# The output projection of a hybrid encoder layer: three blocks of 512 tokens and columns of 512 against two halves of 768 tokens and columns of 1024

## The chip, the core and the metric

The kernel runs on one core of a Trainium2 chip. The metric is the device time of one execution in microseconds (us), the median of several runs; less is better. TensorE (PE) multiplies matrices, VectorE (DVE), ScalarE (ACT) and GpSimd (POOL) work on tiles in the on-chip memory, and SyncE (SP) here only issues DMA transfers. The five engines each run their own list of instructions in order and wait for one another by semaphores.

## The reference, cut to what matters

The layer normalises the tokens (1,024 of a prompt and 512 of a sample, 1,536 in all, width 2,048), projects them with `w_in`, runs three kinds of attention, multiplies each branch by a gate and joins them to `y` (1,536 x 2,048). What the change touches is the last line:

```
y = jnp.concatenate([ya, yb, yc], axis=-1) @ w_out     # w_out is 2048 x 2048, float32
return x + rmsnorm(y, post_gain)                       # mean of squares over the 2048 columns of a row
```

The product needs float32 accuracy, so each operand is split into a rounded part H and a remainder L, and a product is the sum of three: H by H, H by L, L by H.

## The kernel before

A first stage multiplies by `w_in` in three passes of 512 tokens (b = 0, 1, 2), then come attention stages, and `y` is left transposed in DRAM (`yT`). The last stage, lines 1546 to 1858, is the output projection, and `low`, `tail` and the pools named in its head are its on-chip memory.

**Tiling.** It goes over three blocks b of 512 tokens, and in each over four column blocks cb of 512. In a block both operands are cut in halves, and seven products (Strassen-Winograd, j = 0 to 6) take the place of eight. On the side of y the operands are A11, A12, S3, S1, S2, A22 and S4 (`OPS`), on the side of the weights two quarters as they are, one more, and four sums of quarters. The contraction of 1,024 is walked in quarters s = 0 to 3, so `columns(b, cb)` has 28 steps (s, j). A step first splits its weights, 128 x 512 numbers (`prep`, line 1680 on ACT makes wH, line 1681 on DVE wL), LEAD = 4 steps ahead, and then runs `product` (line 1689): 2 rows groups q x 2 slices c x 3 matmuls of 256 columns, 12 in all, with y as the stationary operand. The whole stage has 336 steps.

**Sums.** GpSimd makes the weight sums of every (b, cb, s) from freshly loaded weights (lines 1664, 1667, 1670, 1674) and the y sums of every block (line 1585). The y operands of a block stay on chip in split form (lines 1589 and 1590).

**Leaving.** `leave(j)` adds finished products into the result tile z (lines 1715 to 1729), `rows_squares` sums squares (line 1609), `gained` multiplies by the gain, and the rows go to DRAM (line 1739). When a block is through, `finish_load` (lines 1627, 1628), `finish_rows` (line 1634) and `finish_store` (line 1638) read z and x back, scale by one over the root, add x and store the output, spread over the following block. The last column block of the last block runs its seven products one after the other instead (`final`), with a tail written out by hand (`tail_*`).

**Order.** Two timelines, `before` and `after`, map a step to the small jobs that are issued ahead of it or behind it. The loop at the end walks the steps and issues all of it in this order on all engines (`IN_ORDER`); so each engine's list is what the code writes. SP has the loads and stores of the stage, and each of its DMAs also waits for the one eight places earlier in its queue, so at most eight are under way.

## Time and profile before

| what | value |
|---|---|
| runs | 3181.72, 3188.18, 3186.55 us; median 3186.55 us |
| the profiled execution | 3185.0 us, of which its span 3183.2 us |
| busy over the span | PE 2999.4 us (94%), DVE 2390.1 us (75%), ACT 1528.5 us (48%), POOL 962.9 us (30%) |
| the output projection | from 2567.15 us to the end of the span |
| DMA over the span | 649.93 MB, 204 GB/s |

The span is from the first to the last instruction on the chip in one profiled execution. A share of busy time is a mean over stages of different kinds: what bounds the last stage is read in its own stretch of the trace, and the chain of waits names what PE waited for. Moments below are microseconds from the start of the span.

### The profile page before, as it was taken

The page shows a single profiled execution, that of the slowest core. Times are in us where ns is not written, and L with a number is a line of the kernel's source. Part 1 is how long each engine was busy: PE and PEld are TensorE (multiplying, and loading weights), DVE is VectorE, ACT ScalarE, POOL GpSimd, SP SyncE. Part 2 cuts the span into 40 slices and gives each one's busy share as a digit, 9 for nine tenths or more (in the row PEclk, how much of TensorE's full clock was granted, in tenths as well). Part 3 has the DMA queues.
Part 4 walks back from the last instruction along what each step waited for, and adds up shares of the span by engine and source line. Part 5 has one row for each costly group of instructions (what it writes and reads, how often), then busy time and mean ns, then how long its engine had stood idle before and what let it go on. Part 6 is the DMA issues. An engine that isn't in the chain of part 4 may idle for free.

```text
span 3183.2 us, 57740 instructions
## 1 busy us (share of the span) xinstructions
PE 2999.4 (94%) x22030; PEld 2823.9 (89%) x22030; DVE 2390.1 (75%) x3887; ACT 1528.5 (48%) x3028; POOL 962.9 (30%) x607
## 2 busy tenths in 40 slices
...
GB/s 215 145 259 249 270 255 287 315 321 187 239 219 223 263 373 205 211 209 225 212 212 221 141 184 161 132 163 115 110 132 106 163 136 136 126 182 247 141 246 227
DMA packets 412335, 649.93 MB, mean 204 GB/s; under 512 B 38445, under 2 KB 247001, under 8 KB 388761
## 3 DMA queue, kind: packets, MB, share of 16 engines
...
## 4 chain that ended last, share of the span: by engine, by line
PE 63%; DVE 15%; DMA 7%; issue 6%; POOL 6%; ACT 2%; SPq 1%; DVEq 0%; POOLq 0%; ACTq 0%
PE m L453 34%; PE s L1332 5%; PE acc L822 4%; DMA w<-in_w_in_dram 4%; DVE wL L1681 4%; PE acc L1689 4%; PE o L1374 3%; PE acc L904 2%; PE m L269 2%; PE acc L1178 2%; PE pp L1352 2%; DVE wL L177 2%; PE acc L1025 2%; POOL w L429 1%; DVE S L1590 1%
## 5 line engine op out<-in xcount | busy, mean ns | idle before, releaser
L177 DVE TENSOR_TENSOR wL<-w,wH 128x512 fp32r<-128x512 f32 x576 | 451.6, 801 | 193.7 <-ACT wH L176 189.9
L176 ACT CAST wH<-w 128x512 fp32r<-128x512 f32 x576 | 349.2, 618 | 340.3 <-PE m L453 272.1
L1689 PE MATMUL acc<-wH,S 128*128 128x256 f32 x1536 | 306.2, 293 | 0.0
L180 DVE SCALAR_TENSOR_TENSOR wL<-w,wH 128x512 fp32r<-128x512 f32 x288 | 224.6, 790 | 107.8 <-ACT wH L179 104.6
L1681 DVE TENSOR_TENSOR wL<-w,wH 128x512 fp32r<-128x512 f32 x288 | 274.0, 976 | 36.1 <-ACT wH L1680 32.2
L1689 PE MATMUL acc<-wL,S 128*128 128x256 f32 x768 | 231.0, 301 | 70.4 <-DVE wL L1681 70.2
L179 ACT ACTIVATE wH<-w 128x512 fp32r<-128x512 f32 x288 | 178.7, 630 | 204.2 <-PE m L453 153.5
L1680 ACT CAST wH<-w 128x512 fp32r<-128x512 f32 x288 | 174.6, 618 | 205.0 <-PE acc L1689 78.2
L1689 PEld LDWEIGHTS acc<-wH,S 128*128 128x128 f32 x1536 | 259.6, 203 | 0.0
L1689 PEld LDWEIGHTS acc<-wL,S 128*128 128x128 f32 x768 | 155.9, 203 | 80.6 <-DVE wL L1681 80.5
L1689 PE MATMUL acc<-wH,A 128*128 128x256 f32 x1152 | 219.9, 281 | 0.2 <-ACT wH L1680 0.2
L992 POOL DMA_DIRECT2D dk<-kaT x8 | 4.5, 557 | 671.1 <-DMA craw<-cqT 485.2
L1689 PEld LDWEIGHTS acc<-wH,A 128*128 128x128 f32 x1152 | 184.5, 191 | 0.8 <-ACT wH L1680 0.8
L1689 PE MATMUL acc<-wL,A 128*128 128x256 f32 x576 | 164.5, 286 | 18.9 <-DVE wL L1681 18.8
L453 PE MATMUL m<-A12H,wL 128*128 128x256 f32 x576 | 166.7, 289 | 10.8 <-DVE wL L177 10.8
L453 PE MATMUL m<-S3H,wL 128*128 128x256 f32 x576 | 165.7, 288 | 7.8 <-DVE wL L177 6.1
L453 PE MATMUL m<-A22H,wL 128*128 128x256 f32 x576 | 165.4, 287 | 6.5 <-DVE wL L177 6.5
L453 PE MATMUL m<-S2H,wL 128*128 128x256 f32 x576 | 165.1, 287 | 4.1 <-DVE wL L177 4.1
L453 PE MATMUL m<-A12H,wH 128*128 128x256 f32 x576 | 167.5, 291 | 0.0
L453 PE MATMUL m<-A22H,wH 128*128 128x256 f32 x576 | 165.9, 288 | 0.0
L453 PE MATMUL m<-A12L,wH 128*128 128x256 f32 x576 | 165.8, 288 | 0.0
L453 PE MATMUL m<-S1H,wL 128*128 128x256 f32 x576 | 163.3, 284 | 2.2 <-DVE wL L177 2.2
...
## 6 DMA issues: line engine op xcount, KB each, us to landing
w<-w SPq DMA_DIRECT2D x144, 1024.0 KB, 8.1
w<-in_w_in_dram SPq DMA_DIRECT2D x96, 1024.0 KB, 8.6
w<-in_w_out_dram SPq DMA_DIRECT2D x94, 512.0 KB, 6.9
T<-w SPq DMA_DIRECT2D x96, 256.0 KB, 5.4
z<-z SPq DMA_DIRECT2D x38, 512.0 KB, 5.2
h<-hA SPq DMA_DIRECT2D x14, 1024.0 KB, 12.0
w<-T SPq DMA_DIRECT2D x48, 256.0 KB, 2.5
y<-yT SPq DMA_DIRECT2D x22, 512.0 KB, 7.0
```

The source lines that it names most:

```text
L176: nc.scalar.copy(H, src)
L177: engine.tensor_sub(L, src, f(H))
L179: nc.scalar.activation(H, src, AF.Copy, scale=scale)
L180: nc.vector.scalar_tensor_tensor(L, src, scale, f(H), op0=ALU.mult, op1=ALU.subtract)
L269: nc.tensor.matmul(a, lhsT=lhsT, rhs=rhs, start=(c == 0 and i == 0), stop=(c == NC_D - 1 and i == 2))
L453: nc.tensor.matmul(M[j], lhsT=w[:, c, :], rhs=h[:, 4 * i + c, :], start=(i == c == x == 0), stop=(i == 1 and c == 3 and x == 2))
L822: nc.tensor.matmul(a, lhsT=wt[:, c, :], rhs=ht[:, c, :], start=(c == 0 and i == 0), stop=(c == 3 and i == 2))
L1332: nc.tensor.matmul(S[:, c], lhsT=a[:, qs], rhs=b[:, c], start=(i == 0), stop=(i == len(pairs) - 1))
L1374: nc.tensor.matmul(o, lhsT=a[:, vs], rhs=b, start=(kc == 0 and i == 0), stop=(kc == n - 1 and i == 2))
L1680: nc.scalar.copy(H, src)
L1681: nc.vector.tensor_sub(L, src, f(H))
L1689: nc.tensor.matmul(m, lhsT=a[:, c, P * q:P * q + P], rhs=w[:, c, :], start=(first and c == x == 0), stop=(s == 3 and c == 1 and x == 2), s ...
```

## The change

The stage is written anew; the way of splitting, the seven products and the three-matmul product stay.

- **Tokens and columns.** Two halves of 768 tokens are A1 and A2 (t = 0, 1), and two column blocks cb = 0, 1 of 1,024 columns, each again in two halves of 512 (lo, hi). So all 1,536 tokens go through one set of seven products for each cb. A step is (j, cb, c) with c = 0 to 7 a slice of 128 of the contraction, and there are 112 steps. A step has 6 row groups q x 3 matmuls of 512 columns, 18 in all, and one split of 128 x 512 weights, LEAD = 2 steps ahead. The products come in three groups: j = 0 and 1 for both cb, then 4, 3 and 6, then 2 and 5.
- **Resident sums of y.** Three slots hold y operands in split form, each replaced piece by piece once its last step is through: slot 0 A11, then S1, then A22; slot 1 A12, then S4, then the last eight weights; slot 2 S2, then S3. The sums are made on GpSimd, 768 wide, in buffers of a ring of four (`y_raw`): S3, S1 and S2 of one c in steps 18, 20, ..., 32, where S2 also goes to DRAM through GpSimd's own DMA queue (`s2_store`); S4 in steps 36 to 46 with S2 read back; S3 again in steps 60 to 74.
- **Weight sums.** They are made once, on GpSimd, in the third pass of the `w_in` stage, every 18 steps of that pass for one of 16 pieces (`out_load`, `out_sums`, `out_store`), and lie in DRAM (`WO`).
- **Partial results.** j = 0, 4 and 3 leave partial results a, U and W (6 row groups x 512 columns for each cb) in DRAM; `load_part` brings them back for the products that add to them. `keep` sums squares, multiplies by the gain and stores a finished piece of z.
- **Finishing.** The first half's rows are finished in steps 81 to 94, from operand buffers that are free by then; the second half's rows after the last products, which run row group by row group (steps 104 to 111 for q = 0, then for q = 1, ...), each followed by its own `leave`, `inverse` and `finish`.

Taken from the diff, cut to its core:

```diff
+    WO = [[scratch(f"wo{n}{cb}", (P, 8 * 512)) for n in range(4)] for cb in range(2)]
...
+        def out_load(cb, c):
+            WOT[cb, c] = t = ring("wo", 2, 1024)
+            for k in range(2):
+                r = 1024 * k + P * c
+                nc.sync.dma_start(t[:, k, :], w_out[r:r + P, 1024 * cb:1024 * cb + 1024])
+            if c % 4 == 0:
+                WOT[cb, "t3"] = ring("wo3", 4, 512)
+        def out_sums(cb, c, i):
+            lo, hi = slice(0, 512), slice(512, 1024)
+            t, t3 = WOT[cb, c], WOT[cb, "t3"][:, c % 4, :]
+            sub = nc.gpsimd.tensor_sub
+            if i == 0:
+                sub(t3, t[:, 1, hi], t[:, 0, hi])
+            elif i == 1:
+                sub(t[:, 0, lo], t[:, 0, hi], t[:, 0, lo])
+            elif i == 2:
+                sub(t[:, 0, hi], t[:, 1, hi], t[:, 0, lo])
+            else:
+                sub(t[:, 1, lo], t[:, 1, lo], t[:, 0, hi])
+        def out_store(cb, c):
+            t = WOT.pop((cb, c))
+            for n, src in ((0, t[:, 0, :512]), (1, t[:, 0, 512:]), (3, t[:, 1, :512])):
+                nc.sync.dma_start(WO[cb][n][:, 512 * c:512 * c + 512], src)
+            if c % 4 == 3:
+                nc.sync.dma_start(WO[cb][2][:, 512 * c - 1536:512 * c + 512], WOT[cb, "t3"].rearrange("p c n -> p (c n)"))
...
+            if b == 2:
+                for i in range(16):
+                    s = start + 20 + 18 * i
+                    before.put(s, out_load, i // 8, i % 8)
+                    for k in range(4):
+                        before.put(s + 7 + 2 * k, out_sums, i // 8, i % 8, k)
+                    before.put(s + 15, out_store, i // 8, i % 8)
...
-        zp = ph.enter_context(pool(name="zp", bufs=4))
-        rp = ph.enter_context(pool(name="raws", bufs=6))
-        wp = ph.enter_context(pool(name="quarters", bufs=6))
+        wp = ph.enter_context(pool(name="w_raw", bufs=4))
+        hp = ph.enter_context(pool(name="w_parts", bufs=3))
+        yp = ph.enter_context(pool(name="y_raw", bufs=4))
+        zp = ph.enter_context(pool(name="z_out", bufs=6))
+        slots = {0: ph.enter_context(pool(name="slot0", bufs=1))}
+        gp = ph.enter_context(pool(name="stats", bufs=1))
+        LEAD, HT, NQ = 2, 768, 6
...
+        def y_sum(out, x, y, c, sign=-1, at=None):
+            o = RAW[at or y, c]
+            (nc.gpsimd.tensor_add if sign > 0 else nc.gpsimd.tensor_sub)(o, RAW[x, c], RAW[y, c])
+            RAW[out, c] = o
+        def y_split(n, slot, c, engine=nc.vector):
+            A[n, c] = slots[slot].tile([P, 2, HT], F32R, tag=f"s{slot}{c}", name=n)
+            H, L = A[n, c][:, 0], A[n, c][:, 1]
+            nc.scalar.copy(H, RAW[n, c])
+            engine.tensor_sub(L, RAW[n, c], f(H))
+        def s2_store(c):
+            nc.gpsimd.dma_start(s2_raw[P * c:P * c + P, :], RAW["S2", c])
+        def s2_load(c):
+            RAW["S2", c] = yp.tile([P, HT], F32, tag="y", name="y")
+            nc.sync.dma_start(RAW["S2", c], s2_raw[P * c:P * c + P, :])
...
+        def w_source(j, cb, c):
+            if j in (0, 1, 6):
+                r = P * c + 1024 * (j > 0)
+                col = 1024 * cb + 512 * (j == 6)
+                return w_out[r:r + P, col:col + 512]
+            return WO[cb][{2: 2, 3: 0, 4: 1, 5: 3}[j]][:, 512 * c:512 * c + 512]
...
+        def w_split(s):
+            j, cb, c = order[s]
+            if s >= n_steps - 8:
+                t = slots[1].tile([P, 2, 512], F32R, tag=f"s1{c}", name="wHL")
+            else:
+                t = hp.tile([P, 2, 512], F32R, tag="w", name="wHL")
+            nc.scalar.copy(t[:, 0], WR[s])
+            nc.vector.tensor_sub(t[:, 1], WR.pop(s), f(t[:, 0]))
+            WS[s] = t
...
+        def product(s, q):
+            j, cb, c = order[s]
+            if c == 0 and FIRST[j] == j:
+                BK[q] = ps.tile([P, 512], F32, tag="acc", name="acc")
+            y, w = A[OPS[j], c], WS[s]
+            t = slice(P * q, P * q + P)
+            for x, (a, b) in enumerate(((0, 0), (1, 0), (0, 1))):
+                nc.tensor.matmul(BK[q], lhsT=y[:, a, t], rhs=w[:, b], start=(c == 0 and x == 0 and FIRST[j] == j),
+                                 stop=(c == 7 and x == 2), skip_group_check=True)
...
+        def keep(t, q, k, st):
+            squares(t, q, k, st)
+            nc.vector.tensor_mul(st, st, Z["gain", k])
+            if (t, k) != (1, 2):
+                nc.sync.dma_start(z_all[HT * t + P * q:HT * t + P * q + P, 512 * k:512 * k + 512], st)
+        def leave(s, q):
+            j, cb, c = order[s]
+            st = zp.tile([P, 512], F32, tag="z", name="z")
+            lo, hi = 2 * cb, 2 * cb + 1
+            if j in (0, 1):
+                nc.scalar.copy(st, BK[q])
+                if j:
+                    keep(0, q, lo, st)
             else:
...
+                part_in = Z["a" if j in (3, 4, 6) else "W" if j == 2 else "U", cb, q]
+                nc.vector.tensor_add(st, part_in, BK[q])
+                if j in (2, 5, 6):
+                    keep(j != 6, q, lo if j == 5 else hi, st)
+            if j in (0, 3, 4):
+                nc.sync.dma_start(part[{0: "a", 4: "U", 3: "W"}[j]][cb][P * q:P * q + P, :], st)
+            return st
...
+        def finish_load(t, q, tags):
+            z, x = (slots[int(n[1])].tile([P, 1536], F32, tag=n, name="tail") for n in tags)
+            rest = yp.tile([P, 512], F32, tag="y", name="rest")
+            r = slice(HT * t + P * q, HT * t + P * q + P)
+            for a, b, o in COLS:
+                nc.sync.dma_start(z[:, o:o + b - a], z_all[r, a:b])
+                nc.sync.dma_start(x[:, o:o + b - a], rows_of(t, q)[0][:, a:b])
+            nc.sync.dma_start(rest, rows_of(t, q)[0][:, 1024:1536])
+            if t == 0:
+                st = zp.tile([P, 512], F32, tag="z", name="zr")
+                nc.sync.dma_start(st, z_all[r, 1024:1536])
+                Z["own", t, q] = st
+            Z["fin", t, q] = z, x, rest
...
+            if split:
+                u = slice(1024, 1536)
+                nc.scalar.activation(z[:, u], z[:, u], AF.Copy, scale=v)
+                nc.gpsimd.tensor_add(z[:, u], z[:, u], x[:, u])
+                stt(own, own, v, rest, op0=ALU.mult, op1=ALU.add)
+                nc.sync.dma_start(out[:, 1024:1536], own)
+                u = slice(0, 1024)
+                stt(z[:, u], z[:, u], v, x[:, u], op0=ALU.mult, op1=ALU.add)
+            else:
+                stt(own, own, v, rest, op0=ALU.mult, op1=ALU.add)
+                nc.sync.dma_start(out[:, 1024:1536], own)
+                stt(z, z, v, x, op0=ALU.mult, op1=ALU.add)
...
+        order = [(j, cb, c) for js in ((0, 1), (4, 3, 6), (2, 5)) for cb in range(2) for j in js for c in range(8)]
+        n_steps = len(order)
+        at = {x: i for i, x in enumerate(order)}
+        for s in range(n_steps):
+            before.put(max(s - 5, -8 + s // 2), w_load, s)
+            before.put(s - LEAD, w_split, s)
+        for c in range(8):
+            for n, slot, first in (("A11", 0, at[0, 0, c]), ("A12", 1, at[1, 0, c])):
+                before.put(first - 4, y_load, n, c)
+                before.put(first - 2, y_split, n, slot, c)
+            s = at[0, 1, 0] + 2 * c
+            for n in ("A11", "A21", "A22"):
+                before.put(s, y_load, n, c)
+            before.put(s + 2, y_sum, "S3", "A11", "A21", c, -1, "A11")
+            before.put(s + 2, y_sum, "S1", "A21", "A22", c, 1, "A21")
+            before.put(s + 2, y_sum, "S2", "A22", "S3", c)
+            before.put(s + 2, s2_store, c)
+            before.put(s + 3, y_split, "S2", 2, c)
+            before.put(s + 3, y_split, "S1", 0, c)
+            s = at[4, 0, 0] + 2 + 3 * c // 2
+            before.put(s, y_load, "A12", c)
+            before.put(s, s2_load, c)
+            before.put(s + 2, y_sum, "S4", "A12", "S2", c)
+            before.put(s + 3, y_split, "S4", 1, c)
+            s = at[4, 1, 0] + 2 + 2 * c
+            before.put(s, y_load, "A11", c)
+            before.put(s, y_load, "A21", c)
+            before.put(s + 2, y_sum, "S3", "A11", "A21", c)
+            before.put(s + 3, y_split, "S3", 2, c)
+            s = at[3, 1, 7] + 3 + c
+            before.put(s, y_load, "A22", c)
+            before.put(s + 2, y_split, "A22", 0, c)
+        for cb in range(2):
+            for q in range(NQ):
+                before.put(at[4, cb, 1 + q // 2], load_part, "a", cb, q)
+                before.put(at[2, cb, 4 + q // 2], load_part, "W", cb, q)
+                before.put(at[5, cb, 4 + q // 2], load_part, "U", cb, q)
+            for j, k in ((1, 2 * cb), (6, 2 * cb + 1), (2, 2 * cb + 1), (5, 2 * cb)):
+                before.put(at[j, cb, 2], load_gain, k)
+        s = at[2, 0, 0]
+        before.put(s + 1, inverse, 0, 0, NQ)
+        for q in range(NQ):
+            tags = [f"s1{2 * (q % 4) + i}" for i in range(2)]
+            before.put(s + 1 + 2 * q, finish_load, 0, q, tags)
+            before.put(s + 4 + 2 * q, finish, 0, q)
+            tags = [f"s2{2 * (q % 4) + i}" for i in range(2)]
+            if q < 4:
+                before.put(at[5, 1, 0] + 1 + q, finish_load, 1, q, tags)
...
+                if 0 <= t < n_steps - 8:
+                    c = order[t][2]
+                    for q in range(NQ):
+                        product(t, q)
+                        if c == 7:
+                            leave(t, q)
...
+            for t in range(n_steps - 7, n_steps + 20):
+                before.run(t)
+            done = None
+            for q in range(NQ):
+                for t in range(n_steps - 8, n_steps):
+                    product(t, q)
+                st = leave(n_steps - 1, q)
+                Z["own", 1, q] = st
+                inverse(1, q, 1)
+                finish(1, q, q == NQ - 1)
+                if q < 2:
+                    finish_load(1, q + 4, [f"s2{2 * q + i}" for i in range(2)])
```

The lists of three engines at the places that matter. In all of them the name left of the arrow is written and the one right of it is read. First GpSimd in the middle of the stage, before: w are weight tiles, T the fourth weight sum.

```order
L1664 TENSOR_TENSOR T_31171<-w 128x512
L1667 TENSOR_TENSOR w<-w 128x2x256
L1670 TENSOR_TENSOR w<-w 128x2x256
L1674 TENSOR_TENSOR w<-w 128x2x256
L1664 TENSOR_TENSOR T_31314<-w 128x512
L1667 TENSOR_TENSOR w<-w 128x2x256
```

And GpSimd in steps 18 to 33 of the changed kernel: y are buffers of the ring of four, and s2raw is in DRAM.

```order
L1612 TENSOR_TENSOR y_31241<-y_31241,y_31243 128x768
L1612 TENSOR_TENSOR y_31243<-y_31243,y_31245 128x768
L1612 TENSOR_TENSOR y_31241<-y_31245,y_31241 128x768
L1622 DMA s2raw_30627<-y_31241 128x768
L1612 TENSOR_TENSOR y_31303<-y_31303,y_31305 128x768
L1612 TENSOR_TENSOR y_31305<-y_31305,y_31307 128x768
L1612 TENSOR_TENSOR y_31303<-y_31307,y_31303 128x768
L1622 DMA s2raw_30627<-y_31303 128x768
```

The weight sums have left GpSimd's list here; three sums of y and a store stand in their place for each c, and the third sum is written over the first.

SP's loads of y in a block before, with what each waits for (DMAHW and DMASW are earlier DMAs, of SP's and of GpSimd's queue):

```order
L1655 DMA w_32300<-in_w_out_dram 128x2x512 [waits DMAHW7_49,Activation_49,Pool_49]
L1655 DMA w_32302<-in_w_out_dram 128x2x512 [waits DMAHW0_49,Activation_49]
L1577 DMA y_32426<-yT0_130 128x2x512 [waits DMAHW1_49]
L1577 DMA y_32428<-yT2_132 128x2x512 [waits DMAHW2_49]
L1655 DMA w_32447<-in_w_out_dram 128x2x512 [waits DMAHW3_49,DVE_49,Pool_49]
```

And in steps 20 to 24 of the changed kernel (line 1607 loads A11, A21 and A22 of one c, line 1639 a step's weights):

```order
L1607 DMA y_31303<-yT0_130 128x768 [waits DMASW6_49]
L1607 DMA y_31305<-yT0_130 128x768 [waits DMAHW7_49,DMAHW3_49,Pool_49]
L1607 DMA y_31307<-yT2_132 128x768 [waits DMAHW4_49,DMASW7_49,DVE_49]
L1639 DMA w_31330<-in_w_out_dram 128x512 [waits DMAHW5_49]
L1639 DMA w_31359<-in_w_out_dram 128x512 [waits DMAHW6_49]
L1607 DMA y_31365<-yT0_130 128x768 [waits DVE_49]
L1607 DMA y_31367<-yT0_130 128x768 [waits DMAHW4_49,DMAHW0_49,Pool_49]
L1607 DMA y_31369<-yT2_132 128x768 [waits DMAHW1_49,DMASW0_49,DVE_49]
```

With four buffers and three loads for each c, the third load of a c now goes into the buffer from which the c before it stored S2 (the wait on DMASW).

SP's list at the last column block, before (tail is where z and x are read back):

```order
L1655 DMA w<-in_w_out_dram 128x2x512 x8
L1638 DMA out_dram<-z 128x2x512
L1659 DMA gain<-in_post_gain_dram 128x512
L1739 DMA z<-z 128x2x512
L1627 DMA tail<-z 128x2x512
L1628 DMA tail<-in_x_sample_dram 128x2x512
```

And after, from the stores of z that belong to step 103 to the first partial results U (rest is a third piece of x):

```order
L1689 DMA z<-z 128x512 x6
L1639 DMA w<-wo_142 128x512 x2
L1722 DMA tail<-z 128x1024
L1723 DMA tail<-in_x_prompt_dram 128x1024
L1722 DMA tail<-z 128x512
L1723 DMA tail<-in_x_prompt_dram 128x512
L1724 DMA rest<-in_x_prompt_dram 128x512
L1639 DMA w<-wo_142 128x512
L1677 DMA gain<-in_post_gain_dram 128x512
L1722 DMA tail<-z 128x1024
```

The stage's last three loads of weights now stand behind six stores of z, and the last of them behind a whole `finish_load` too; the loads of U come two more `finish_load` later.

## Rows read from the trace of the kernel before

**Rows 1.** Windows: from:to, length, busy by engine (count), PEclk, DMA share, GB/s

```profile
2567.15:3171.58 604.43, 514.84 (x4033) 499.46 (x4031) 557.75 (x594) 283.19 (x528) 390.56 (x237) 0.95 0.54 180
3171.58:3183.20 11.62, 0.00 (x1) 0.00 (x0) 6.29 (x11) 2.25 (x5) 3.47 (x2) 0.60 0.58 218
```

**Rows 2.** What PE waited for, 2567 to 3160: us in total, times, longest

```profile
PE acc L1689 <- DVE wL L1681: 86.6, 58, 5.0
```

**Rows 3.** Chain that ended last: start, length, engine and line, matmuls in a row

```profile
1303.45 172.79 PE m L453 x1440
...
1853.63 2.74 PE acc L822 x12
...
2843.02 36.84 PE acc L1689 x299
```

**Rows 4.** DVE by line, 2567 to 3184: busy, mean ns | idle before, releaser

```profile
L1681 DVE TENSOR_TENSOR wL<-w,wH 128x512 fp32r<-128x512 f32 x286 | 271.6, 974 | 36.1 <-ACT wH L1680 32.2 <-DMA out_dram<-z 1.2
...
L1722 DVE TENSOR_TENSOR z<-z,acc 128x512 f32<-128x512 f32 x12 | 8.2, 687 | 0.4
```

**Rows 5.** ACT by line, 2567 to 3184

```profile
L1680 ACT CAST wH<-w 128x512 fp32r<-128x512 f32 x285 | 172.8, 618 | 203.8 <-PE acc L1689 78.2 <-POOL w L1667 47.9 <-POOL w L1670 37.3
L1609 ACT ACTIVATE junk<-z 128x512 f32<-128x512 f32 (+1 forms) x50 | 30.7, 614 | 28.0 <-DVE z L1727 12.7 <-DVE zss L1607 7.5 <-DVE z L1719 5.3
...
L1609 ACT ACTIVATION_READ_ACCUMULATOR junk<-z 128x1 f32 x50 | 9.3, 186 | 0.0
```

**Rows 6.** POOL by line, 2567 to 3184, then 1900 to 2560 by form

```profile
L1585 POOL TENSOR_TENSOR y<-y 128x512 f32<-128x512 f32 x44 | 78.6, 1787 | 37.5 <-DVE A L1590 36.5
...
L1309 POOL TENSOR_TENSOR vL<-hraw,vH 128x1024 fp32r<-128x1024 f32 x8 | 19.3, 2418 | 74.6 <-ACT vH L1308 74.6
```

**Rows 7.** DMA issues, 1700 to 2560, then the page: KB each, us to landing

```profile
hraw<-knT SPq DMA_DIRECT2D x7, 512.0 KB, 5.5
hraw<-qnT SPq DMA_DIRECT2D x8, 256.0 KB, 2.9
yT<-y SPq DMA_DIRECT2D x23, 256.0 KB, 2.1
yT<-dy SPq DMA_DIRECT2D x4, 512.0 KB, 3.3
...
L992 POOL DMA_DIRECT2D dk<-kaT x8 | 4.5, 557 | 671.1 <-DMA craw<-cqT 485.2
```

**Rows 8.** DMA in 3080 to 3184: 40 slices of GB/s, one issue

```profile
GB/s 217 269 225 0 210 331 277 215 387 269 317 283 333 268 405 243 7 3 0 0 0 3 273 268 358 405 403 392 386 388 351 17 32 169 352 285 286 279 210 0
...
tail<-in_x_sample_dram SPq DMA_DIRECT2D x8, 512.0 KB, 10.7
```

**Rows 9.** Timeline of the end: start, length, engine and line

```profile
3173.08 0.41 DVE L1779 TENSOR_TENSOR z<-z,acc 128x256 f32<-128x256 f32 x1
...
3175.66 0.16 DVE L1621 RECIPROCAL zs<-zs 128x1 f32<-128x1 f32 x1 [0.36 <-ACT zs L1614]
...
3179.39 0.38 SPq L1758 DMA_DIRECT2D out_dram<-tail  x1
```

**Rows 10.** Passes of the `w_in` stage: DVE by line in the third, windows, waits

```profile
L177 DVE TENSOR_TENSOR wL<-w,wH 128x512 fp32r<-128x512 f32 x179 | 122.6, 691 | 87.4 <-ACT wH L176 85.9
...
180.00:660.00 480.00, 455.97 (x3648) 445.14 (x3648) 388.48 (x545) 205.73 (x365) 261.62 (x166) 0.99 0.79 277
1220.00:1690.00 470.00, 470.00 (x3925) 470.00 (x3924) 294.57 (x506) 226.13 (x387) 1.41 (x3) 1.00 0.61 206
...
PE m L453 <- DVE wL L177: 11.3, 8, 4.7
...
PE m L453 <- DVE wL L180: 3.3, 3, 1.8
```

**Rows 11.** DMA issues of the page: KB each, us to landing

```profile
w<-w SPq DMA_DIRECT2D x144, 1024.0 KB, 8.1
```

294 lines of the change are left out of this document (47 added, 247 removed).

## Prediction

> **What bounds the kernel now.** I read the windows first. The stage runs from 2567.15 to 3171.58, 604.4 us, and 11.6 us follow the last matmul [rows 1]. In it PE and DVE are both busy nearly throughout (515 and 558 us), ACT is not, and DMA runs at 180 GB/s, half of what it reaches near the end. PE's waits say what it lacks: 86.6 us in 58 waits, all for wL, the remainder of a weight split [rows 2]. The chain of waits gives the pace of PE itself: 299 matmuls of 256 columns in 36.84 us, .123 each, and 12 of 512 columns in 2.74, .228 each [rows 3]. The stage's granted clock was .95, and these rates hold it. 4,032 x .123 = 497; with the waits 584 of the 604. Of DVE's work the remainders are the largest item, 286 shown at 974 ns [rows 4], and they are what PE waits for. So the stage is PE's stream plus a shortage of DVE.
>
> **The stream of products.** It becomes 112 steps of 18 x .228 = 4.11 us, 460 in all instead of 497. There are 112 weight splits instead of 336, .62 + .97 us a step [rows 4, 5] against 4.11: the steady wait for wL goes. What is late next is no longer an engine's sum but single places, so I followed the changed lists step by step and asked of each what ends last. T16 is the start of step 16.
>
> Start: the first A11 piece needs PE's last `w_in`-side work to be through, then cast, remainder and a weight split, 2.7 us in all. 104 steps then give 104 x 4.11 = 427.4.
>
> **The loop of y sums, steps 18 to 36.** GpSimd makes S3, S1 and S2 of a c and stores S2; the load of A22 of the next c goes into that buffer, so it waits for the store to land; S1 and S2 of the next c need that A22. This loop has no slack and one turn of it, P, is: issue of the store .56, landing 2.7 (2.1 for 256 KB, 3.3 for 512 KB), landing of the load 4.2 (2.9 and 5.5) [rows 7], two sums 768 wide, and .4 for semaphores. A sum is bounded by 768/1024 x 2.418 = 1.8 where GpSimd had DVE off its back, and 1.5 x 1.787 = 2.7 in this stage [rows 6]; I take 2.3, the middle, since DVE is busy here for less than half the time. P = .56 + 2.7 + 4.2 + 4.6 + .4 = 12.5, against 8.2 for the two steps in which the list offers it. The ends are 9.5 (all low) and 15.2 (all high).
>
> What hangs on the loop: on ACT and DVE the split of S2 stands in line, and the weight split of step 22 + 2c stands behind it. S2 of c = 0 is done at T16 + 18, as its loads stand behind six stores of z on SP; two turns lack the wait for a store (c = 1 and 5, .9 shorter each), so S2 of c = 6 is done at T16 + 16.2 + 6P. Behind it on ACT are its cast (.9), the six copies and squares of `leave` 31 (6 x (.62 + .80) = 8.5 [rows 5]), the split for step 34 (1.6), then steps 34 and 35 (8.2), and .6 for semaphores: step 36 starts 19.8 later. Without waits it would start at T16 + 82.2. The loss is 16.2 + 6P + 19.8 - 82.2 = 6P - 46.2 = 29; 11 at P = 9.5 and 45 at 15.2.
>
> The row shows 1,787 ns for a GpSimd sum of 512 columns here, and half of 2,418 = 1,209 where it reads the same width elsewhere [rows 6]; DVE's remainder takes 691 ns in the third `w_in` pass, where GpSimd rests [rows 10], and 974 here [rows 4]. The Trainium skill ("SBUF — State Buffer", section "SBUF: two separate sides") says that DVE and GpSimd share a port pair as an exclusive lock, and that a transfer issued by GpSimd waits for its descriptors while DVE holds the pair, 620 ns becoming about 3,100. The sums agree with the lock; no row here shows a store from GpSimd's queue under it. With 2.5 us added to the store, an estimate from that page, P would be 15.0 and the loss 44.
>
> **Leaving.** `keep` (j = 2, 5, 6) runs on DVE for each of six row groups: add .69, wait for ACT's square .71, product with the gain .69 [rows 4, 5], 2.2 with semaphores, 13.2 for six, while PE's next step wants banks and splits from the same engines. At steps 55 and 79 two or three steps of lead cover most of it, and I charge 2 each. At 87 and 95 it meets the finishing of the first half: in steps 80 to 98 SP carries 28.4 MB (six stores of z 1.6, six `finish_load` of 2.1 each, six stores of rows of 1.05, fifteen weights, W and U 3.1, y .8), all in one queue. At the .39 MB/us of the fastest slices of the present tail [rows 8] that is 73 us from T80 + 10 on, when `leave` 79 has let its stores go; the last parts of U, which `leave` 95 needs, are near its end, and step 98 comes at T80 + 89 against 73.8: 15. This and the two leaves make 19. At .30 MB/us it would be 18 more.
>
> **The end.** `keep` of step 103 runs until T104 + 9.8, and its six stores stand ahead of the weights 109 and 110 on SP; a whole `finish_load` (1.8 MB) stands ahead of weight 111. Since the last group runs q by q, the first q needs all eight weights: it ends at about T104 + 20 instead of 5.5, and PE at 20 + 5 x 5.5 = T104 + 47.5. The first U stands behind 6.8 MB: 10 + 6.8/.39 + 1.5 = T104 + 29. From there DVE does row group after row group: add to reciprocal 2.8 (3175.66 + .16 - 3173.08 [rows 9]), the own piece .7, a 1,536 wide piece 1.9 (below three times .69, as it is one instruction; 2.5 by six times the .41 of 256 columns), 5.4 in all. The sixth starts at 29 + 5 x 5.4 = 56; +2.8, +2.5 for the last scaling and sum on ACT and GpSimd, +3.8 for the last store (3183.20 - 3179.39 [rows 9]): T104 + 65. With everything in time it would be 32.9 for the stream and 11.6 as now [rows 1].
>
> **The third pass of `w_in`.** It gains 64 sums, at most 64 x 1.787 = 114 us of GpSimd [rows 6], and 33.6 MB in 470 us, 71 GB/s on top of 206. The first pass is the same work with much of both beside it: GpSimd 262 us busy, DMA 277 GB/s, and DVE 388 against 295 us; it lost 11.3 + 3.3 us in waits for wL, and is 10 us longer than a third pass without a wait [rows 10]. Loads of weights are issued eight steps ahead (8 x 12 x .12 = 11.5 us [rows 3]) and land in 8.1 [rows 11]. GpSimd's load is some 40% of the first pass's, and DVE's is less: I charge 3, between 0 and 24 (both kinds of wait and the 10 us). It can't gain: PE is busy there without a gap.
>
> **The sum.** 2567.15 + 2.7 + 427.4 + 29 + 19 + 65 + 3 = 3113.3. The profiled execution was 3185.0 for a span of 3183.2, and the median 3186.55: 1.8 + 1.5 on top give 3116.6, so 3117, 70 us (2.2%) less.
>
> **Rivals.** A, PE sets the pace all through: the loop's turn is near its low end, banks and lead hide the leaves, and the last weights are early. Then 2567.15 + 2.7 + 460.3 + 11 (the loop) + 14 (the end, a little over today's 11.6) + 3.3 = 3059. For it speaks that ACT and DVE have less than half of the old work and that transfers in this trace often land in 2 to 3 us; against it, that all the waits named are written into the lists' order. B, GpSimd and DVE shut each other out, or the stores wait for DVE: two sums of 2.7, and a store that lands as late as the slowest load of rows 7, 5.5 like the load: P = .56 + 5.5 + 5.5 + 5.4 + .4 = 17.4, a loss of 58 instead of 29, 3146. For it speak 1,787 against 1,209 and 974 against 691; against it, that DVE is busier in the old stage than it will be. C, slower: the loop's transfers land as the tail's did under full load, 10.7 us [rows 8], both store and load: P = .56 + 10.7 + 10.7 + 5.4 + .4 = 27.8, loss 121, 3117 - 29 + 121 = 3209. It decides from the loss at which 70 us are gone, 99, so from P = 24.2. Against it, the loop moves only some 1.5 MB a turn plus weights, far below the rate of that tail. D, the third pass costs its whole 24: 3138, inside the range. That the change doesn't do what it says is ruled out by the lists: 2,016 matmuls of 512 columns and 112 weight splits stand in them.
>
> **How the numbers follow.** Forecast with its own spread (the loop 11 to 45, the queue at .39 or .30, the third pass 0 to 24) 55%: 3085 to 3142; A 18%, B 19%, C 8%. The range that holds eight in ten takes the forecast, B and the upper part of A: 3062 to 3165. 0.2%, 6.4 us, is about what can be told from no change here. Faster by more: all but C and a mixture of B with D, 90%; within: 3%; slower: 7%.
>
> **What would show it.** In the trace of after: matmuls of .228 and a step of 4.11 between the waits; PE's waits for wL gone from the steady part; between steps 20 and 36 waits of PE for weight splits of about 29 us, with A22 loads released by GpSimd's stores and turns of about 12.5; waits near step 88 and 96 for the adds of `leave`, with SP's queue full; the last matmul some 47 us and the end some 65 us after the start of step 104; PE in the third pass as full as now. The forecast is wrong if turns are near 8 (A), near 17 (B) or above 24 (C), if the U parts come as asked, or if GpSimd's sums in the third pass hold DVE up.

## The result, and the profile after

| | median of the runs | ratio to before, 95% interval | span of the profiled execution |
|---|---|---|---|
| before | 3186.41 us | | 3183.2 us |
| after | 3131.89 us (3131.4 to 3135.12) | .9833 (.9816 to .985) | 3133.3 us |

54.5 us less by the medians, where 70 were forecast; the time lies 15 us above the forecast and inside the range. The sum of the prediction was for the span, 3113.3, and the span is 3133.3. Twenty microseconds have to be found in its terms, and the terms that seem right have to be shown to be so. The profiled execution of after is the slowest of its four (3135.12 us; the others lie at 3131.4 to 3132.3), so some 3 of the twenty are that one execution's.

What bounded the stage before was PE's wait for the remainder of a weight split, 86.6 us up to 3160 [rows 2] and 89.0 to the end. The same view of after, from 2567.2 to the end (engine, line, what it waited for: us, times, longest):

```profile
PE acc L1661 <- DVE z L1701: 20.8, 12, 7.1
PE acc L1661 <- ACT z L1696: 18.9, 2, 10.0
PE acc L1661 <- ACT wHL L1647: 14.2, 6, 7.8
PE acc L1661 <- DVE wHL L1648: 1.5, 1, 1.5
PE acc L1661 <- DVE A L1619: 0.8, 1, 0.8
```

56 us in 22 waits instead of 89 in 59, and remainders (line 1648) are hardly among them. What is left are single places: banks that `leave` has not yet copied out (line 1696, two waits) or added out (line 1701), and weights at the end (line 1647). PE's own timeline shows where (start, length, matmuls in one run, and in brackets the idle time before the run and what ended it):

```profile
2567.67 100.60 PE L1661 MATMUL acc<-wHL,A 128*128 128x512 f32 x431 [0.79 <-DVE A L1619]
2678.22 36.68 PE L1661 MATMUL acc<-wHL,A 128*128 128x512 f32 x144 [9.95 <-ACT z L1696]
...
2725.36 9.32 PE L1661 MATMUL acc<-wHL,S 128*128 128x512 f32 x32 [8.93 <-ACT z L1696]
2736.21 94.75 PE L1661 MATMUL acc<-wHL,S 128*128 128x512 f32 x409 [1.53 <-DVE wHL L1648]
...
2837.26 58.49 PE L1661 MATMUL acc<-wHL,S 128*128 128x512 f32 x252 [0.43 <-ACT wHL L1647]
2896.32 36.64 PE L1661 MATMUL acc<-wHL,S 128*128 128x512 f32 x156 [0.57 <-DVE z L1701]
2933.23 0.96 PE L1661 MATMUL acc<-wHL,S 128*128 128x512 f32 x3 [0.26 <-DVE z L1701]
...
2979.09 1.65 PE L1661 MATMUL acc<-wHL,A 128*128 128x512 f32 x3 [6.29 <-DVE z L1701]
2987.87 1.65 PE L1661 MATMUL acc<-wHL,A 128*128 128x512 f32 x3 [7.13 <-DVE z L1701]
...
3058.65 1.55 PE L1661 MATMUL acc<-wHL,A 128*128 128x512 f32 x6
3068.05 4.21 PE L1661 MATMUL acc<-wHL,A 128*128 128x512 f32 x9 [7.85 <-ACT wHL L1647]
...
3080.26 30.51 PE L1661 MATMUL acc<-wHL,A 128*128 128x512 f32 x123 [3.62 <-ACT wHL L1647]
```

Counting 18 matmuls to a step gives every run its step: 2678.22 is step 24, 2736.21 step 34, 2933.23 row group 4 of step 80, the two waits of 6.29 and 7.13 are row groups 3 and 4 of step 88, and 3058.65 is step 104. (The stage's first matmul, at 2566.38, is not in these lines: with it 431 are 24 x 18 = 432. Step 34 is counted from its third matmul, as PE waited ahead of that one.)

**The pace.** The runs without a wait tell what a matmul costs. Windows over the 299 matmuls of before [rows 3], from which I had taken .123, and over three places of after (from:to, length, busy by engine, granted clock, DMA share, GB/s):

```profile
2843.02:2846.40 3.38, 3.38 (x16) 3.38 (x17) 3.38 (x6) 0.62 (x1) 0.00 (x0) 0.54 0.40 147
2846.40:2875.80 29.40, 29.40 (x255) 29.40 (x254) 27.52 (x31) 12.90 (x21) 18.75 (x12) 1.00 0.88 296
```

```profile
2678.22:2684.40 6.18, 6.18 (x15) 4.88 (x16) 1.57 (x2) 2.90 (x6) 2.06 (x2) 0.50 0.67 237
2684.40:2714.90 30.50, 30.50 (x132) 24.61 (x131) 11.88 (x12) 8.65 (x13) 16.11 (x11) 1.00 0.74 230
2736.21:2831.00 94.79, 94.75 (x409) 76.76 (x409) 38.62 (x52) 22.04 (x37) 15.27 (x8) 1.00 0.60 198
```

The run of before began behind a wait of 3.43 us, and PE's clock was at .54 in its first stretch, near the lower of the two levels, 1.2 GHz; then it was 1.00, and 252 matmuls took 29.4 us, .1167 each. In after 409 of 512 columns took 94.75 us, .2317 each, .1158 for 256 columns. And a wait of PE costs more than its length: behind the 9.95 us before step 24 the clock was at .50 for 6.18 us, which cost 2.9 us beside the wait.

The start times of all matmuls of the stage in the two traces give the pace of the whole. A distance between two starts counts here as full pace up to .13 us (256 columns) or .245 us (512), as slow up to .24 or .485, and above that as a gap. At full pace the mean is .1173 us before (3,663 of 4,031 distances) and .2310 after (1,899 of 2,015), .1155 for 256 columns. So the wide matmuls made PE 1.5% faster: all products at that pace are 473 us before and 465 after. The whole stage, with what follows it, is then (rounded):

| us | before | after |
|---|---|---|
| PE's products at full pace | 473 | 465 |
| what slow matmuls (286 and 84) take beyond it | 27 | 14 |
| waits of PE that the profile names | 89 | 56 |
| the rest of the gaps between matmuls | 15 | 7 |
| from the last matmul on | 12 | 23 |
| start of the stage to the end of the span | 616 | 566 |

The slow matmuls run at about half the full pace (.21 and .40 us on average), as in the two windows above with the clock at .50 and .54. The gain in the two profiled executions is 33 us of named waits, 13 of slow matmuls, 8 of other gaps and 7 of pace, less 11 at the end: 50 us.

### The profile page after: what moved, and what is told of

Read it like the earlier page. It is cut to its first block, busy times and chain, and to the rows that moved or that the text cites. A ratio compares the mean times of both kernels' runs of the same rounds, so it can differ in the third digit from the quotient of the medians.

```text
span 3133.3 us, 53258 instructions
## 1 busy us (share of the span) xinstructions
PE 2971.1 (95%) x20014; PEld 2710.0 (86%) x20014; DVE 2099.4 (67%) x3591; ACT 1395.3 (45%) x2782; POOL 726.5 (23%) x470
## 4 chain that ended last, share of the span: by engine, by line
PE 69%; DMA 11%; DVE 8%; POOL 4%; issue 4%; ACT 2%; SPq 1%; DVEq 0%; POOLq 0%; ACTq 0%
PE m L454 34%; PE acc L1661 8%; PE s L1371 5%; PE acc L861 5%; DMA w<-in_w_in_dram 4%; PE o L1413 3%; PE m L270 2%; PE acc L943 2%; PE acc L1217 2%; PE pp L1391 2%; PE acc L1064 2%; DVE wL L178 1%; DMA h<-hA 1%; POOL w L430 1%; POOL T L427 1%
## 5 line engine op out<-in xcount | busy, mean ns | idle before, releaser
L178 DVE TENSOR_TENSOR wL<-w,wH 128x512 fp32r<-128x512 f32 x576 | 465.6, 829 | 174.7 <-ACT wH L177 171.6
L177 ACT CAST wH<-w 128x512 fp32r<-128x512 f32 x576 | 348.2, 618 | 335.2 <-PE m L454 264.0
L1661 PE MATMUL acc<-wHL,S 128*128 128x512 f32 x1152 | 272.6, 397 | 16.5 <-ACT z L1696 8.9
L1661 PEld LDWEIGHTS acc<-wHL,S 128*128 128x128 f32 x1152 | 216.1, 189 | 72.6 <-ACT z L1696 10.1
L1661 PE MATMUL acc<-wHL,A 128*128 128x512 f32 x864 | 215.8, 413 | 40.9 <-DVE z L1701 16.4
L1661 PEld LDWEIGHTS acc<-wHL,A 128*128 128x128 f32 x864 | 170.2, 199 | 86.3 <-DVE z L1701 19.2
L454 PE MATMUL m<-A12H,wL 128*128 128x256 f32 x576 | 166.6, 289 | 11.7 <-DVE wL L178 11.7
L454 PE MATMUL m<-S3H,wL 128*128 128x256 f32 x576 | 166.1, 288 | 9.7 <-DVE wL L178 7.9
L454 PE MATMUL m<-S2H,wH 128*128 128x256 f32 x576 | 165.3, 287 | 0.0
L454 PE MATMUL m<-S4H,wL 128*128 128x256 f32 x576 | 163.2, 283 | 1.8 <-DVE wL L181 1.8
L454 PE MATMUL m<-S3H,wH 128*128 128x256 f32 x576 | 164.8, 286 | 0.0
L861 PE MATMUL acc<-c,sH 128*128 128x512 f32 x480 | 160.6, 416 | 3.9 <-ACT c L833 2.3
```

The source lines that it names most:

```text
L177: nc.scalar.copy(H, src)
L178: engine.tensor_sub(L, src, f(H))
L454: nc.tensor.matmul(M[j], lhsT=w[:, c, :], rhs=h[:, 4 * i + c, :], start=(i == c == x == 0), stop=(i == 1 and c == 3 and x == 2))
L861: nc.tensor.matmul(a, lhsT=wt[:, c, :], rhs=ht[:, c, :], start=(c == 0 and i == 0), stop=(c == 3 and i == 2))
L1661: nc.tensor.matmul(BK[q], lhsT=y[:, a, t], rhs=w[:, b], start=(c == 0 and x == 0 and FIRST[j] == j), stop=(c == 7 and x == 2), skip_group_ ...
```

## The experiments

All are read by the same marks in their profiles: S, the start of the first long run of products; the start of step 34; row group 4 of step 80; step 104; the end. S itself lies between 2561 and 2571 in these profiles, with the same code ahead of it, so medians that differ by less than some 6 us say little and the stretches say more. They have a spread too: the end took 74.6 to 76.1 us in the four kernels of the table in which its code is that of after (after, no_round_trip, own_ring, no_first_finish).

| kernel | S to 34 | 34 to 80 | 80 to 104 | 104 to end | median, us | ratio to before |
|---|---|---|---|---|---|---|
| after | 168.5 | 197.0 | 125.4 | 74.7 | 3131.9 | .9833 |
| no_round_trip | 154.3 | 196.2 | 127.1 | 76.1 | 3122.1 | .9808 (.9788 to .9828) |
| own_ring | 166.1 | 196.2 | 121.2 | 74.6 | 3123.0 | .9812 (.9794 to .983) |
| u_first | 168.1 | 197.0 | 125.3 | 75.1 | 3132.6 | .9837 (.9819 to .9855) |
| half_columns | 174.3 | 199.2 | 124.8 | 74.0 | 3138.7 | .9851 (.9832 to .987) |
| three_splits_b | 177.2 | 217.2 | 132.8 | 77.6 | 3173.2 | .9968 (.9957 to .998) |
| no_first_finish | 167.8 | 197.0 | 108.7 | 76.1 | 3115.9 | .9782 (.9768 to .9795) |
| all_four | 155.6 | 196.2 | 122.5 | 71.1 | 3116.1 | .9786 (.9772 to .9801) |
| all_five | 155.2 | 196.2 | 122.5 | 71.3 | 3116.6 | .9788 (.9775 to .9801) |

### The weight sums alone

The kernel before, and in its third `w_in` pass the new `out_load`, `out_sums` and `out_store`:

```diff
+            if b == 2:
+                for i in range(16):
+                    s = start + 20 + 18 * i
+                    before.put(s, out_load, i // 8, i % 8)
...
+                    before.put(s + 15, out_store, i // 8, i % 8)
```

> The kernel before, with only one part of the change added: the 64 weight sums, their loads and their stores in the third pass of the w_in stage (33.6 MB, 64 sums on GpSimd); nobody reads their results. Theory: PE has slack for them, since DVE rises from 295 to about 329 busy us of 470 and PE stays busy without a gap: 0 to +3 us against the kernel before. Rival (the third pass becomes like the first): waits for wL of 10 us and more appear there, and the time rises by 10 to 24 us.

3187.3 us, ratio 1.0009 (1.0 to 1.0019): between 0 and 6 us. The window over the pass:

```profile
1220.00:1690.00 470.00, 469.72 (x3918) 469.34 (x3917) 335.03 (x505) 225.26 (x386) 101.40 (x68) 1.00 0.81 276
```

DVE is 40 us busier than [rows 10] and GpSimd 100 us, and PE still has no gap. The remainder of that pass took 815 ns here and 808 in the changed kernel instead of 691, and the trace shows where that comes from: the 175 remainders of this window during which no GpSimd sum ran took .69 us each, the 35 that met one 1.48. DVE has the room for it. The part is nearly free, as charged (3).

### The loop of y sums without the round trip through DRAM

```diff
-            before.put(s + 2, s2_store, c)
...
-            before.put(s, s2_load, c)
-            before.put(s + 2, y_sum, "S4", "A12", "S2", c)
+            before.put(s + 2, s4_sum, c)
...
+        def s4_sum(c):
+            o = RAW["S4", c] = RAW["A12", c]
+            for k in range(2):
+                nc.gpsimd.tensor_sub(o, o, f(A["S2", c][:, k]))
```

> The changed kernel, but S4 is made on GpSimd from the resident split form of S2 (A12 minus H minus L, two sums instead of one), so that S2 is neither stored nor loaded back. Theory: in steps 18 to 36 the turn of 11.5 us is set by the landing of the store and of the load that waits for it; without the store the turn is load 4 + two sums 3.6 + some 0.8, at most 8.4, the two waits of PE near steps 24 and 32 (10.0 and 8.9 us) fall to 4 or less together, and the time falls by 14 to 20 us against the changed kernel. Rival (GpSimd's sums beside DVE, or the copies in ACT's line, set the turn): it stays above 10.5 us and the time within 4 us.

The loop of the changed kernel first, GpSimd's timeline of two turns (start, length; in brackets its idle time and what ended it):

```profile
2672.53 3.56 POOL L1612 TENSOR_TENSOR y<-y 128x768 f32<-128x768 f32 x2 [2.39 <-DMA y<-yT]
2676.38 0.56 POOL L1622 DMA_DIRECT2D s2raw<-y  x1 [0.30 <-POOL y L1612]
2679.76 1.83 POOL L1612 TENSOR_TENSOR y<-y 128x768 f32<-128x768 f32 x1 [2.82 <-DVE S L1619]
2684.17 3.63 POOL L1612 TENSOR_TENSOR y<-y 128x768 f32<-128x768 f32 x2 [2.58 <-DMA y<-yT]
2688.10 0.56 POOL L1622 DMA_DIRECT2D s2raw<-y  x1 [0.30 <-POOL y L1612]
```

From store to store 11.7 us; over the six turns from the first store, 2654.67, to the seventh, 2723.52, 11.5. What PE waits for at steps 24 and 32 are ACT's copies of finished banks (line 1696), and in ACT's list these stand behind the cast of S2, which waits for the loop:

```profile
2676.12 1.56 ACT L1618 CAST S<-y 128x768 fp32r<-128x768 f32 x2 [8.98 <-POOL y L1612]
2677.59 3.02 ACT L1696 COPY z<-acc 128x512 f32<-128x512 f32 x6
```

And without the store:

```profile
2655.00 1.86 POOL L1612 TENSOR_TENSOR y<-y 128x768 f32<-128x768 f32 x1 [3.18 <-DMA y<-yT]
...
2664.34 5.98 POOL L1612 TENSOR_TENSOR y<-y 128x768 f32<-128x768 f32 x3 [3.29 <-DMA y<-yT]
...
2673.51 1.83 POOL L1612 TENSOR_TENSOR y<-y 128x768 f32<-128x768 f32 x1 [3.19 <-DMA y<-yT]
```

9.2 a turn (2655.00 to 2673.51 is two; 9.6 over all seven turns), not the 8.4 expected: each turn still waits for loads into buffers that the c before must free (SP's loads of y wait 27 us for GpSimd's sums and 10 for DVE's splits between 2640 and 2720). PE's two waits fell from 10.0 and 8.9 us to

```profile
2672.45 35.23 PE L1666 MATMUL acc<-wHL,A 128*128 128x512 f32 x144 [5.75 <-ACT z L1701]
...
2711.96 0.96 PE L1666 MATMUL acc<-wHL,S 128*128 128x512 f32 x3 [2.88 <-ACT z L1701]
```

so to 8.9 with a wait of .3, where 4 or less were expected. The stretch to step 34 is 14.2 us shorter, the median 9.8, where 14 to 20 were expected. The store and the load behind it set the turn; that they are all of the loss was too much. That S2 can be had from its own split parts, for one more sum of some 2.2 us each, is by the stretches the largest improvement found.

### The finishing of the first half

```diff
-            tags = [f"s1{2 * (q % 4) + i}" for i in range(2)]
+            tags = [f"s1{2 * (q % 3) + i}" for i in range(2)]
...
-                st = zp.tile([P, 512], F32, tag="z", name="zr")
+                st = slots[1].tile([P, 1536], F32, tag=f"s1{6 + q % 2}", name="zr")[:, :512]
```

> The changed kernel, but the piece of z that the finishing of the first half reads back (zr) lies in two buffers of slot 1 of its own, no longer in the ring of six that the leaving results use (three rows in flight instead of four). Theory ring: the two waits of leave 87 (6.3 and 7.1 us at step 88) are for buffers of that ring; they go, and the time falls by 10 to 13 us against the changed kernel. Theory queue, which is the one of the prediction: steps 80 to 98 are paced by 28.4 MB on SP's queue at .39 MB/us; the waits only move to the parts of U before step 96, step 98 comes as late as now, and the time falls by 0 to 3 us.

DVE's timeline of the changed kernel names what the two long waits at step 88 are:

```profile
2978.35 0.69 DVE L1701 TENSOR_TENSOR z<-zW,acc 128x512 f32<-128x512 f32 x1 [5.70 <-DMA out_dram<-zr]
...
2987.13 0.69 DVE L1701 TENSOR_TENSOR z<-zW,acc 128x512 f32<-128x512 f32 x1 [6.55 <-DMA z<-z]
```

The add of a leaving result needs a buffer of the ring of six, and that buffer still holds a finished row on its way out, or an earlier z. With its own buffers for zr the waits of step 88 fell from 16.4 us to 6.5. But 80 to 104 is only 4.2 us shorter: at step 96 the waits rose from 2.2 to 6.1, led by

```profile
3006.11 1.00 PE L1661 MATMUL acc<-wHL,S 128*128 128x512 f32 x3 [4.00 <-DVE z L1701]
```

This wait is for an add that stands in DVE's list behind the scaling of a finished row, and that one waited for the load of its zr:

```profile
3002.38 0.75 DVE L1745 SCALAR_TENSOR_TENSOR zr<-zr,zinv,rest 128x512 f32<-128x512 f32 x1 [4.92 <-DMA zr<-z]
```

Neither theory alone: the wait is for the ring, as theory ring says, and much of what is won there is lost at the next place, as theory queue says, though not at the parts of U. From 2968 to 3005 us the DMA engines were busy throughout, at 375 GB/s, so a late load is what a full queue would give; own_ring also has one row less in flight, and no run separates the two. The median is 8.9 us lower. The two profiled executions differ by 13.9 us, of which 6.5 are an earlier S and 7.4 lie in the stretches. To see what the finishing costs in all, it was left out:

```diff
-            before.put(s + 1 + 2 * q, finish_load, 0, q, tags)
-            before.put(s + 4 + 2 * q, finish, 0, q)
```

> The changed kernel without the finishing of the first half: the rows of tokens 0 to 767 are neither read back nor scaled nor stored, so that part of the output is missing; all else stays. In the changed kernel steps 80 to 104 take 125 us, where 24 steps of 4.17 are 100. Theory: the finishing is what costs the 25 (its bytes on SP's queue, and the six buffers of z that it shares): 16 to 23 us less than the changed kernel, with 3 to 9 left for the adds of the leaves at 80, 88 and 96. Rival (the leaves themselves cost it): 6 us less or nothing.

80 to 104 fell by 16.7 us to 108.7, and the median by 16. So the finishing costs 17; the other 8 or so are the adds of the leaves (7.3 us of named waits at steps 80, 88 and 96 are left).

### The end

First the order of loads: the six parts of U and their gain ahead of the second half's loads.

```diff
-                before.put(at[5, cb, 4 + q // 2], load_part, "U", cb, q)
+                before.put(at[5, cb, 0 if cb else 4 + q // 2], load_part, "U", cb, q)
```

> The changed kernel, but the last six loads of U and their gain stand right behind the stores of z of step 103, ahead of the loads for finishing the second half. Theory: the first row group waits for its U until 32.2 us after the start of step 104 while its products end at about 23; with U early the rows start at 23 to 24, the row chain of 5.25 us each follows, and the end comes 7 to 9 us earlier. Rival (the bytes on SP's queue set the end): the last weights now stand behind U too, the rows' loads come as late, and the time stays within 3 us.

Nothing: 75.1 instead of 74.7. The first row group did start its add earlier, 28.3 us after step 104 instead of 32.2, and the last one lost it again. In the changed kernel that last row reads (DVE's timeline):

```profile
3117.07 0.68 DVE L1701 TENSOR_TENSOR z<-zU,acc 128x512 f32<-128x512 f32 x1
...
3121.18 1.35 DVE L1740 SCALAR_TENSOR_TENSOR z<-z,zinv,rest 128x512 f32<-128x512 f32 x1 [1.29 <-DMA rest<-in_x_sample_dram]
```

and in u_first:

```profile
3113.67 0.69 DVE L1701 TENSOR_TENSOR z<-zU,acc 128x512 f32<-128x512 f32 x1 [0.16 <-PE acc L1661]
...
3120.56 1.17 DVE L1740 SCALAR_TENSOR_TENSOR z<-z,zinv,rest 128x512 f32<-128x512 f32 x1 [4.07 <-DMA rest<-in_x_sample_dram]
```

The bytes count too, as the rival said: the last weights, now behind U, came later, PE's waits for them grew from 12.9 to 18.3 us, and the products ended 56.4 us after the start of step 104 instead of 52. But the end is set by the last row, which waits for its x, and that load is late since row groups 4 and 5 are read into the buffers of 0 and 1 and so wait for those to be stored. SP's timeline of the changed kernel shows the line in which they stand (line 1749 stores, lines 1722 to 1724 load):

```profile
3096.19 0.82 SPq L1749 DMA_DIRECT2D out_dram<-tail  x2
3101.14 0.33 SPq L1722 DMA_DIRECT2D tail<-z  x1
...
3104.42 0.93 SPq L1749 DMA_DIRECT2D out_dram<-tail  x2
3112.71 0.33 SPq L1722 DMA_DIRECT2D tail<-z  x1
...
3124.16 1.89 SPq L1749 DMA_DIRECT2D out_dram<-tail  x2
```

Store, 4 us, load, store, 7 us, load (SP's two waits in line 1722 are for stores of tail, 11.4 us in all): a chain that a faster first row doesn't shorten much. I formed a theory of slots and tested it from both ends. The weights early too:

```diff
-            before.put(s - LEAD, w_split, s)
+            before.put(s - LEAD if early < 0 else 101 + (0, 0, 1, 1, 1, 2, 2, 2)[early], w_split, s)
```

> The changed kernel with U and its gain ahead of the second half's loads (as in u_first), and the last eight weights loaded in steps 99 to 103 and split in steps 101 to 103, ahead of the stores of step 103. Theory slots: the end hangs on a chain through SP's queue, where the loads of row group 4 wait for the landed stores of row group 0 and those of 5 for the stores of 1; the first row group is finished at about 23 us after the start of step 104 instead of 36, and the chain of store 9, load 3, store 9, load 3 + 7, finish 3 and store 9 from there ends at about 66 instead of 74.7: 7 to 11 us less than the changed kernel. PE ends some 34 us after the start of step 104 instead of 52. Theory PE and rows (what the first group waits for moves the end one to one): 13 to 18 us less.

PE was through 33.2 us after the start of step 104 (3053.74) instead of 52, and the end came after 75.7 (with 1.5 us more in steps 80 to 104, where the early weights now stand): 3130.9 us, ratio .9824 (.9806 to .9841), no gain. Both theories had expected some: the first row was finished at 29, not at 23, since its x and the gain came late, and each link of the chain took as long as the stores and loads under way let it. Then row group 4 in buffers that wait for nobody:

```diff
+            if tags is None:
+                z, x, h = (hp.tile([P, 1024], F32, tag="w", name="tail") for _ in range(3))
+                rest = wp.tile([P, 512], F32, tag="w", name="rest")
...
-                if q < 2:
-                    finish_load(1, q + 4, [f"s2{2 * q + i}" for i in range(2)])
+                if q < 1:
+                    finish_load(1, 5, ["s20", "s21"])
```

> As u_w_first, but the second half's row group 4 is read into the three buffers of split weights and one of raw weights, which are free by then, so its loads wait for no store, and row group 5 takes the place of row group 0. Theory slots: one turn of the chain (store 9 and load 3) falls away: the end is 55 to 58 us after the start of step 104, 8 to 11 us less than u_w_first, 16 to 20 less than the changed kernel. Theory bytes (the 20 MB after step 103 at .39 MB/us set it): 3 us or less below u_w_first.

70.9 us after step 104, 4.8 less than u_w_first, where slots asked for 8 to 11 and bytes for 3 or less; 3126.8 us, ratio .9815 (.9795 to .9835). The window over the end of rows_first says why no order of issue is likely to bring much more:

```profile
3064.00:3115.00 51.00, 20.91 (x92) 16.82 (x90) 24.33 (x37) 6.82 (x19) 1.26 (x1) 0.75 0.94 341
```

For 51 us the DMA engines are 94% busy. After step 103 there are six z stores (1.6 MB), six U (1.6), six rows of z and x (11) and six of output (6.3), 20.5 MB, which at .341 MB/us is 60 us of the 71 (50 at the .40 to .41 of the fastest slices of the end). So bytes are most of the end, with 10 to 20 us of the chain on top. That is read from the window: no run moved fewer bytes.

### How much of the gain is the width, and how much the number of splits

Each product as two of 256 columns:

```diff
-                nc.tensor.matmul(BK[q], lhsT=y[:, a, t], rhs=w[:, b], start=(c == 0 and x == 0 and FIRST[j] == j),
+                for h in (slice(0, 256), slice(256, 512)):
+                    nc.tensor.matmul(BK[q][:, h], lhsT=y[:, a, t], rhs=w[:, b, h],
```

> The changed kernel, but each matmul of 512 columns is made as two of 256 with the same stationary operand: 4,032 instead of 2,016, as many as before the change. Theory: the width alone is worth 2 x .123 - .232 = .014 us for each of 2,016: 28 us more than the changed kernel, a little less where PE waits anyway, so 20 to 28. Rival (width is worth nothing, the whole gain is the waits): within 4 us.

+6.8 us by the medians; in the profiles +5.8 in the first stretch and +2.2 in steps 34 to 80, where 197.0 became 199.2. The median's difference alone is near what can't be told from noise, but the pace agrees: .1174 us at full pace, as before the change (.1173), so 473 us of products for 465. The expectation of 20 to 28 was wrong, because .123 wasn't the pace of 256 columns but that of a run with a slow start. 4,032 narrow matmuls cost 1 to 2% more than 2,016 wide ones.

Each weight split three times over, so that DVE and ACT split as many as before:

```diff
-            nc.scalar.copy(t[:, 0], WR[s])
-            nc.vector.tensor_sub(t[:, 1], WR.pop(s), f(t[:, 0]))
+            for _ in range(3):
+                nc.scalar.copy(t[:, 0], WR[s])
+                nc.vector.tensor_sub(t[:, 1], WR[s], f(t[:, 0]))
+            WR.pop(s)
```

> The changed kernel, but every weight split is made three times over, cast and remainder, so that ACT and DVE split as many weights as before the change (336 times), with the weight sums still made in the third pass of the w_in stage. Theory number of splits (they were too many for DVE, and that made the 86.6 us of waits): waits of PE for splits grow by 50 us and more, and the time by as much. Theory GpSimd (before, its sums in the stage slowed and held up DVE's remainders; the number alone fits into the steps): a step of 4.2 us holds three splits of .69; the waits grow only behind places where DVE or ACT is already late, and the time by 5 to 25 us.

3209.7 us, ratio 1.0073 (1.0055 to 1.009): 78 more than after, slower than before the change. That is too strong a test, since here each cast waits for the remainder ahead of it, and a split lasts three times cast and remainder, some 4.2 us, a whole step. So again with the three casts together and the three remainders behind them:

> As three_splits, but the three casts of a weight split stand together and the three remainders behind them, since in three_splits each cast had to wait for the remainder before it and a split took three such rounds, near the 4.2 us of a step by itself. Now ACT needs 1.9 and DVE 2.1 us of each step. Theory number of splits: the waits of PE still grow by 50 us or more against the changed kernel, and the time by as much. Theory GpSimd (before the change its sums held up DVE, the number alone fits): the time grows by 10 to 30 us, by waits behind places where ACT or DVE is late already.

3173.2 us: 41 more than after, between the two expectations. Its waits:

```profile
PE acc L1664 <- DVE z L1704: 33.1, 20, 6.5
PE acc L1664 <- ACT z L1699: 16.9, 2, 12.4
PE acc L1664 <- DVE wHL L1650: 16.3, 13, 4.1
PE acc L1664 <- ACT wHL L1648: 12.9, 3, 9.1
```

The waits for remainders are back, 13 of them: four in the loop of y sums (8.8 us), three behind leaves (4.0) and six at the last eight weights (3.5). Named waits grew by 25 us; the other 16 are slow matmuls (10) and gaps that the profile doesn't name. So three splits for one, in this arrangement, take back 41 of the 54 us. That is no share to set off against GpSimd's sums: the same number in the other arrangement took back 78, and of the 89 us of waits for remainders this run brings back only 16.

What it leaves out are the sums, and the traces show what those did to DVE (duration of the remainders in ns, least/median/most; of before, three_splits_b and after, and last an add of before whose second operand comes from an accumulator):

```profile
L1681 DVE TENSOR_TENSOR wL<-w,wH x288: 656/683/1810, 2561.4 to 3164.6; 128x512 fp32r<-128x512 f32 x144
L1650 DVE TENSOR_TENSOR wHL<-w,wHL x336: 678/692/2335, 2563.2 to 3120.4; 128x512 fp32r<-128x512 f32 x168
L1648 DVE TENSOR_TENSOR wHL<-w,wHL x112: 677/692/2311, 2566.1 to 3080.2; 128x512 fp32r<-128x512 f32 x112
L1722 DVE TENSOR_TENSOR z<-z,acc x12: 686/687/689, 2629.0 to 3153.3; 128x512 f32<-128x512 f32 x12
```

Laid over GpSimd's sums, a remainder during which no sum ran took at most .70 us in each of these traces. Of those that took over .75, every one ended .55 us after the end of the sum that was running: 124 before, 27 in three_splits_b, 10 after. Those that met a sum took 1.31 us on average before (184 of 336), 1.47 in three_splits_b (43 of 336) and 1.34 after (17 of 112). The adds that read an accumulator were not lengthened, beside a sum or not (10 of the 12 of line 1722 met one). All in all DVE lost some 198 of its 558 busy us before [rows 1] in this way, 41 in three_splits_b and 17 after. So the change relieved DVE twice, by 224 remainders of .69 us (154 us) and by some 180 us of standing behind sums, and the prediction's sum counted only the first. How the 89 us of waits divide between the two isn't settled: no run has a third of the splits with the weight sums in the stage.

### All together

no_round_trip, own_ring and rows_first in one kernel, and the same with the second half's output stored through GpSimd's queue:

```diff
+            queue = nc.gpsimd if t else nc.sync
...
-                nc.sync.dma_start(out[:, 1024:1536], own)
+                queue.dma_start(out[:, 1024:1536], own)
```

> no_round_trip, own_ring and rows_first together. If their gains add up: 10 + 4 to 9 + 5 us less than the changed kernel, so 3108 to 3113. If what one gives is taken back at the next place, where SP's queue carries the same bytes: 3117 or more.

> all_four, and the stores of the second half's finished rows go out on GpSimd's DMA queue instead of SP's, so that they stand in no line with the loads and GpSimd, which is idle then, issues them. Theory slots (stores and loads wait for each other in one line): 3 to 6 us less than all_four. Theory bytes (the DMA engines are full then): within 2 us. Rival: stores that GpSimd issues beside DVE's work come late, as it needs the memory port that DVE holds: slower than all_four by 3 us or more.

3116.1 and 3116.6 us: 15 to 16 less than the changed kernel, 2.1% less than before. For all_four this lies between the two expectations (its runs reach from 3111 to 3122), so the medians decide neither; the stretches add up nearly whole (12.9 + .8 + 2.9 + 3.6 by all_four's row, where the three kernels by themselves gave 14.2, 4.2 and 3.8). The second queue changes nothing (71.3 for 71.1), as theory bytes said: the line in which the stores stand doesn't set the end, nor are stores from GpSimd's queue late.

## Why the prediction came out as it did, point by point

- **The stream of products.** Wrong in its reason. The 460 us for after are near the 465 at full pace, but I priced 256 columns at .123 and 512 at .228 and so credited the width with 37 us. The two paces don't compare: the .123 holds the low clock behind a wait, the .228 is from twelve matmuls in a row. At full pace the kernels need 473 and 465 us, and half_columns shows the same 7. What I took for the width were slow matmuls behind waits and gaps that the profile doesn't name; that half of them went with the waits was luck. The steady wait for remainders went, as said, but for a reason of which I had named half: fewer splits, and no weight sums of GpSimd beside them.
- **104 steps at 4.11.** This term was mis-sized by 21 us: 3058.65 - 2567.67 = 491.0, less 42.6 of waits, leaves 448.4, 4.31 a step. By the starts of the matmuls 5 of the 21 are the full pace (4.16 a step), some 10 slow matmuls such as those at the start of step 24, and 6 gaps beyond the named waits.
- **The loop.** The turn and its links were right: 11.5 where 12.5 was said. With it the sum 6P - 46.2 gives 22.8, and 9.95 + 8.93 + 1.53 = 20.4 were lost, where 29 was said. The place was not: I expected PE to wait for weight splits ahead of step 36, and 18.9 of the 20.4 us are waits at steps 24 and 32 for copies of banks, which stand behind the cast of S2 on ACT. A sum took 1.8, the low bound; the store's landing 4.2, above the 2.7 taken; the load after it 3 to 4. On the Trainium skill ("SBUF — State Buffer", section "SBUF: two separate sides"): by the estimate drawn from its figure for late descriptors of a transfer that GpSimd issues, the turn would have been 15.0. That figure is for a copy on DVE; by the same section a sum or difference of two tensors in SBUF, which is what DVE runs here, was not seen to hold such a transfer up. The stores (384 KB) landed in 4.2 us, and loads of the same size on SP's queue took 3.7 in the same steps, so no such delay is seen. Its lock does show, on DVE's side: a difference of two tensors in SBUF stands still until the sum is through, and one with an operand from an accumulator does not. In the loop it cost GpSimd's sums little: they took 1.79 to 1.94 us each, with DVE 31% busy.
- **Leaving, steps 80 to 98.** The size was right by chance. Waits of 1.9 + 16.4 + 2.2 at steps 80, 88 and 96 stand against 15. The step named was the U parts behind 28.4 MB; they were not late (DVE's first add of zU, at 3020.29, waited for nothing, and the 2.2 us are the adds themselves). The ring of z buffers held step 88, which I hadn't priced beyond 6.6. own_ring shows the next limit right behind it, the load of a finished row. The sum beside it was off as well: 28.4 MB at .30 MB/us are 22 us more than at .39, not 18.
- **The end.** PE's end was right within 5 us (T104 + 52 for 47.5), the first add was at 32.2 for 29, and the rows took 5.25 each for 5.4. Mis-sized was the last store: 3133.3 - 3124.2 = 9.1 us with others under way, where I took the 3.8 of a quiet tail; and the last x came 1.3 late. With 2.4 by which the sixth row began late and .5 in its scaling that is 9.5 of the 9.7. The reason behind it was incomplete: I saw U and the weights as the cause, and the two runs that brought them forward gained nothing, because the reuse of two buffers comes next, and behind it most likely the 20 MB.
- **The third pass.** 0 for 3, and sums_alone bounds it to 0 to 6.
- **The sum.** 3113.3 + 21.0 (pace) + 9.7 (end) - 5.4 (waits: 42.6 for 48) - 5.2 (S at 2567.7 for 2572.9, inside the spread of S) = 3133.4, the span. So the forecast is 20 and not 31 us off because errors of both signs met, and no rival had the largest of them, the pace.
- **The rivals.** A fell: PE was not through the loop or the end without waits. B's and C's turns (17.4, 27.8) were not seen; what B says of DVE is true of the old stage, but not of the loop. D did not happen.

What stays open: what the fewer splits and the absent sums each take of the 89 us of waits; whether fewer bytes would shorten the end; and why three splits a step, at 2.4 of its 4.2 us on DVE, still make PE wait.
